# Decoder layer on one core: new places among the products for the small steps of twelve attention units, and other engines for some scalings and splits

## The chip, the cores and the metric

The kernel runs on one core of a Trainium2 chip. The metric is the device time of one execution in microseconds (us), lower is better. The core has five engines with a queue of instructions each: PE (TensorE, the products), DVE (VectorE), ACT (ScalarE), POOL (GpSimd) and SP (SyncE, which here starts the DMA transfers). Each engine takes its own instructions strictly in order and waits on semaphores for the others.

## The reference, cut to what matters

One decoder layer on x of 1024 tokens by 1024 channels, float32:

```python
h = rms_norm(x, ln_pre_mix)
proj = h @ w_in
u_pool, q, k, v = parts of proj            # 256 channels pooled, 12 heads of 64
q, k = rope(q, pos), rope(k, pos)
pool_out = multi_scale_pool(u_pool, w_pool, pool_scale)
for window, dilation in ((128, 1), (512, 4), (2048, 16)):
    o, lse = dilated_branch(q, k, v, window, dilation)   # blocks of 128, band of two blocks
attn_out = sum of the three o, weighted by softmax of the three lse
x = x + rms_norm(concat(pool_out, attn_out) @ w_out, ln_post_mix)
h = rms_norm(x, ln_pre_ffn)
x = x + rms_norm((silu(h @ w_gate) * (h @ w_up)) @ w_down, ln_post_ffn)
```

The change touches the attention alone, in the first 420 us or so. The feed-forward half behind it has the same instructions in the same order before and after.

## The kernel before

**Units.** The twelve heads are six pairs. A unit is a pair and a part h: units 0, 2, 4, 6, 8, 9 are h=0 of pairs 0 to 5 (the branch with dilation 4, called dense here, 5 score steps and 8 scalings), units 1, 3, 5, 7, 10, 11 are h=1 (the other two branches together, 8 score steps and 16 scalings). Each unit goes through the same stages:

- scores: PE makes q k products into a bank `ps_s`; DVE reduces the bank to the row maximum and leaves the shifted scores in the tile `pp` (L761 for dense, L827 for the rest); ACT takes exp (L764, L830).
- merge, for h=1 alone: DVE makes `ex` (L853), PE multiplies it by a selection matrix, and a chain of small DVE steps (L866 to L883) ends in the weights `wv`.
- weigh: each 128x256 piece of `pp` is multiplied by its weight, on DVE (L912), ACT (L910) or POOL (L914), as the table `wx` says (0 POOL, 1 DVE, 2 ACT). The dense units scale by `wd` (L770, then L894 to L898).
- turns: PE transposes four pieces of `pp` into a bank `ps_t` (L295); ACT copies it into `ptr` (L965), and DVE subtracts that copy from the bank (L966), which gives the low half.
- products: PE multiplies both halves of `ptr` by v into `ps_o`. At the end ACT takes the lower rows out (`low`, L1009), DVE adds them (L1010), and `mix` is written (L924, L926).

**Fill.** Between these steps PE does the projections of the pairs to come (`ps_pj`), three products for each 128 channels. The weight for them is split into a high half by ACT (L336) and a low half by DVE or POOL (L340; DVE in one instruction of 128x1024, POOL in two of 128x512), into tiles `whl`. What comes out of a projection of k or q is turned by position: a shuffle (L529) and a multiplication by cos (L530) on DVE, a multiplication by sin (L531) and an addition (L534) on DVE or POOL, then ACT and DVE split the result into `k` (L553, L554) or `qh` and `ql` (L559 to L561).

**What sets the order.** Every step of every unit has a place, a number: 5.4 lies four tenths of the way through unit 5. The table `PRM` (L30 on) holds the places by stage for h=0 and h=1 (`s0`, `s1` the scores, `m` the merge, `w0`, `w1` the weighing, `t0`, `t1` the turns, `v0`, `v1` the products), `du` adds a correction for each unit, and `emit` (L1135) runs all steps in order of place. PE's instructions keep the order in which they were written. For DVE, ACT and POOL a scheduler decides, with a priority for the steps inside `tc.high_priority`; how far ahead these are taken is `hp`, or the entry in `hk` for a stage ('s' reduce and exp, 't' the two halves of `ptr`, 'j' merge) and a unit. `we` says for each w_in tile which engine makes its low half, `r0` to `r3` and `rx` do so for the two multiplying and adding steps of a rotation.

PE has two banks for each of `ps_s`, `ps_t`, `ps_o` and `ps_pj`: a step that wants the third waits until the first has been read.

Of the kernel before, what the change touches and what calls it, by code (L numbers as in the profile page):

```python
# [28 lines left out]

PRM = {'sqe': (0, 0, 0, 0, 1, 1, 0, 1),  # L30
 'sqa': (1, 0, 0, 1, 0, 0, 0, 1),
 'we': (1, 1, 1, 0, 1, 0, 0, 0, 0, 0, 1, 0),
 'nt0': 0.55356,
 'nt1': 0.46388,
 'lag': 3.0,
 'hp': 150,
 'fl': 13,
 'lt': 2.819,
 'ls': 2.439,
 'lm': 2.915,  # L40
 'lw': (4.389, 0.132),
 'nm': 0.03805,
 'n2': 0.00854,
 'n0': 0.101,
 'n1': 0.37349,
 'h0': {'s0': -0.02534,
        's1': 0.41536,
        'm': 0.38673,
        'w0': 0.55,
        'w1': 0.95895,  # L50
        't0': 0.85,
        't1': 1.6,
        'v0': 1.1,
# [1 line left out]
 'h1': {'s0': 0.0,  # L55
        's1': 0.54775,
        'm': 0.61911,
        'w0': 0.77087,
        'w1': 1.33988,
        't0': 0.97415,  # L60
        't1': 1.84152,
# [2 lines left out]
        'u0': 0.15366,  # L64
        'u1': 0.10633,
        'u2': 0.41454,
        'u3': 0.53154},
 'f0': 7e-05,
 'f1': -0.00185,
 'first': {'s0': 0.526,  # L70
           's1': 0.6942,
           'm': 0.79582,
           'w0': 0.75,
           'w1': 0.95,
           't0': 1.09294,
           'v0': 1.3,
           'v1': 1.95},
 'vt': ((1.1002, 1.11456),
        (2.75936, 3.21636),
        (4.7781, 5.38909),  # L80
        (6.79523, 7.29364),
        (8.78599, 10.29739),
        (9.92992, 10.41018)),
 'pw': (-0.11865, -0.09, -0.01308),
 'wp': (1, 1, 1),
 'pb': 0.53585,
 'pe': 0,
 'cut': {7: (1, 12, 9), 9: (1, 10, 17)},
# [188 lines left out]
ON_DVE = ((0, 1),)  # L277
SWAP16 = [(i + 16) % 32 for i in range(32)]
# [1778 lines left out]
```

## Time and profile before

| | |
|---|---|
| median of 3 runs | 1110.48 us (1109.21 to 1111.19) |
| profiled execution | 1109.0 us, with a span of 1107.2 us from the first to the last instruction |
| TensorE clock granted in it | 0.999 |
| busy in the span | PE 99%, DVE 72%, ACT 50%, POOL 47% |

The profiled execution lies 1.5 us below the median and just under the lowest of the three runs. A row of the timeline has the start in us, the time from the first start to the last end of the row's instructions in us, the engine, the line, the operation, what it writes and reads, the shape, and the number of instructions (x4); a bracket at the end is idle time of the engine just ahead, and what ended it. Neighbouring products overlap: one of 128x512 is shown as 0.39 us long and the next starts 0.23 us after it. A row of the waits has the engine, what it was about to do, what it waited for, and then the sum, the number and the longest of these waits.

### The profile page before, as it was taken

How to read it: one execution, taken by the hardware profiler on the slowest of the kernel's cores; microseconds unless marked ns; L12 is line 12 of the kernel's file. 1: busy time of each engine (PE TensorE's matmuls, PEld its weight loads, DVE VectorE, ACT ScalarE, POOL GpSimd, SP SyncE). 2: the span in 40 equal slices, each digit the busy share in tenths (PEclk: the TensorE clock that was granted, in tenths of full speed). 3: DMA queues.
4: the chain of work that ended last, by engine and by line, in shares of the span. 5: the costliest groups of instructions: out<-in, count | busy, mean ns of one | idle time of the engine just before them, and what ended most of it. 6: DMA issues, size and time to landing. Idle time of an engine off the chain costs nothing.

```text
span 1107.2 us, 16032 instructions
## 1 busy us (share of the span) xinstructions
PE 1094.3 (99%) x5653; PEld 930.8 (84%) x5653; DVE 798.0 (72%) x1356; ACT 550.8 (50%) x985; POOL 524.8 (47%) x425
## 2 busy tenths in 40 slices
PE   9999999999999999999999999999999999999998
PEld 7888899989888888888888888888888888888887
DVE  7967978787988767799777777667566476343684
ACT  7456767676777755856322222233222535343432
POOL 0111617263554021100567777586568958666521
PEclk9999999999999999999999999999999999999999
DMA  8225232415149438664476666543445878656442
GB/s 296 95 75 189 95 136 71 159 67 181 53 158 338 146 144 305 226 228 154 158 241 238 238 238 232 205 171 124 152 177 210 281 274 286 205 180 206 134 152 77
DMA packets 91296, 201.81 MB, mean 182 GB/s; under 512 B 9296, under 2 KB 25168, under 8 KB 89808
## 3 DMA queue, kind: packets, MB, share of 16 engines
q1 hardware_dynamic: 90240, 200.00, 51.5%
q8 instruction: 44, 0.72, 0.3%
q10 hardware_dynamic: 976, 0.79, 0.2%
q14 instruction: 36, 0.29, 0.1%
HBM read 143.87 MB, written 56.89 MB: 181 GB/s over the span
## 4 chain that ended last, share of the span: by engine, by line
PE 90%; DVE 4%; ACT 3%; POOL 2%; issue 1%; DMA 0%; ACTq 0%; DVEq 0%; POOLq 0%
PE ps_pj L292 27%; PE ps_s L292 25%; PE ps_o L292 25%; PE ps_t L292 10%; PE ps_t L295 2%; POOL whl L340 1%; ACT ptr L965 1%; ACT pp L830 1%; DVE ptr L966 1%; DVE ql L561 0%; DMA wraw<-in_w_in_dram 0%; DVE pp L912 0%; DVE qh L560 0%; POOL rco L534 0%; DVE rsw L529 0%
## 5 line engine op out<-in xcount | busy, mean ns | idle before, releaser
L292 PE MATMUL ps_o<-tT,fw 128*128 128x512 f32 x648 | 150.4, 389 | 0.0
L292 PEld LDWEIGHTS ps_o<-tT,fw 128*128 128x128 f32 x648 | 121.6, 188 | 25.2
L292 PE MATMUL ps_pj<-x,whl 128*128 128x512 f32 x480 | 131.5, 399 | 0.2 <-DVE whl L340 0.2
L1482 POOL TENSOR_TENSOR fw<-rw,fw 128x512 fp32r<-128x512 f32 x72 | 99.0, 1398 | 32.1 <-ACT fw L1480 30.7
L292 PEld LDWEIGHTS ps_pj<-x,whl 128*128 128x128 f32 x480 | 86.4, 188 | 14.6 <-DVE whl L340 0.7
L340 POOL TENSOR_TENSOR whl<-wraw,whl 128x512 fp32r<-128x512 f32 x44 | 60.3, 1392 | 66.8 <-ACT whl L336 62.1
L1777 POOL TENSOR_TENSOR op<-rw,op 128x512 fp32r<-128x512 f32 x38 | 61.1, 1607 | 39.1 <-ACT op L1776 39.1
L366 POOL TENSOR_TENSOR nrr<-nrr,half 128x4 f32<-128x4 f32 (+1 forms) x7 | 6.9, 988 | 141.1 <-ACT eps L365 99.0
L292 PE MATMUL ps_s<-b,fw 128*128 128x512 f32 x312 | 72.5, 389 | 0.0
L1778 DVE TENSOR_TENSOR op<-rw,op 128x512 fp32r<-128x512 f32 x33 | 45.1, 1368 | 34.5 <-ACT op L1776 32.4
L1776 ACT ACTIVATE op<-rw 128x1024 fp32r<-128x1024 f32 x38 | 40.0, 1059 | 58.6 <-PE ps_t L292 28.6
L292 PEld LDWEIGHTS ps_s<-b,fw 128*128 128x128 f32 x312 | 58.6, 188 | 12.1
L1482 POOL TENSOR_TENSOR whl<-rw,whl 128x512 fp32r<-128x512 f32 x30 | 47.9, 1616 | 43.4 <-ACT whl L1480 29.6
L1480 ACT ACTIVATE fw<-rw 128x1024 fp32r<-128x1024 f32 x45 | 47.5, 1062 | 38.7 <-PE ps_o L292 15.5
L292 PE MATMUL ps_pj<-whl,x 128*128 128x256 f32 (+1 forms) x432 | 64.7, 298 | 0.0
L966 DVE TENSOR_TENSOR ptr<-ps_t,ptr 128x512 fp32r<-128x512 f32 (+1 forms) x84 | 53.0, 647 | 14.5 <-ACT ptr L965 14.1
L965 ACT ACTIVATE ptr<-ps_t 128x512 fp32r<-128x512 f32 (+1 forms) x84 | 45.3, 562 | 32.5 <-PE ps_t L295 23.7
L292 PEld LDWEIGHTS ps_pj<-whl,x 128*128 128x128 f32 x432 | 57.3, 191 | 2.2
L830 ACT ACTIVATE pp<-pp,sx 128x256 f32<-128x256 f32 x96 | 47.9, 501 | 8.1 <-DVE sx L827 7.6
L292 PE MATMUL ps_o<-ptr,v 128*128 128x128 f32 (+3 forms) x376 | 50.6, 268 | 1.2 <-DVE ptr L966 0.8
L1777 POOL TENSOR_TENSOR fw<-rw,fw 128x512 fp32r<-128x512 f32 x26 | 41.6, 1599 | 19.4 <-ACT fw L1776 18.8
L292 PE MATMUL ps_pj<-b,fw 128*128 128x512 f32 x216 | 50.3, 389 | 0.0
(337 smaller groups left out, 2773.9 us busy)
## 6 DMA issues: line engine op xcount, KB each, us to landing
rw<-bd SPq DMA_DIRECT2D x77, 256.0 KB, 4.1
rw<-in_w_gate_dram SPq DMA_DIRECT2D x28, 512.0 KB, 4.7
rw<-in_w_up_dram SPq DMA_DIRECT2D x28, 512.0 KB, 5.6
v<-vd SPq DMA_DIRECT2D x22, 512.0 KB, 4.6
rw<-wsd SPq DMA_DIRECT2D x44, 256.0 KB, 3.9
bd<-p SPq DMA_DIRECT2D x39, 256.0 KB, 2.1
rw<-in_w_down_dram SPq DMA_DIRECT2D x33, 256.0 KB, 4.2
wraw<-in_w_out_dram SPq DMA_DIRECT2D x15, 512.0 KB, 5.7
```

The source lines that it names most:

```text
L292: return tc.keep_in_program_order(nc.tensor.matmul(*a, **k))
L295: return tc.keep_in_program_order(nc.tensor.transpose(dst, src, by))
L340: pin(eng.tensor_tensor(dst[:, 1, at:at + w], src[:, at:at + w], dst[:, 0, at:at + w].bitcast(F32), ALU.subtract))
L366: powers.append(nc.gpsimd.tensor_tensor(r, r, half.to_broadcast([P, n]), ALU.pow))
L830: nc.scalar.activation(pt[:, j, lo:], pt[:, j, lo:], AF.Exp, bias=sx[:, 0, side, j, hd, 0:1], scale=-1.0, accum_out=sx[:, 0, side, j, hd, ...
L965: nc.scalar.activation(ptr[:, 0, :w], t[:, :w], AF.Copy)
L966: nc.vector.tensor_tensor(ptr[:, 1, :w], t[:, :w], ptr[:, 0, :w].bitcast(F32), ALU.subtract)
L1480: nc.scalar.activation(dst[:, :, 0], src, AF.Copy)
L1482: low[0] = eng.tensor_tensor(dst[:, i, 1], src[:, i], dst[:, i, 0].bitcast(F32), ALU.subtract)
L1776: nc.scalar.activation(w[:, :, 0], raw, AF.Copy)
L1777: nc.gpsimd.tensor_tensor(w[:, 0, 1], raw[:, 0], w[:, 0, 0].bitcast(F32), ALU.subtract)
L1778: (nc.gpsimd if p == "P1" else nc.vector).tensor_tensor(w[:, 1, 1], raw[:, 1], w[:, 1, 0].bitcast(F32), ALU.subtract)
```

## The change

Only the table `PRM` changes. Every function stays as it was, and PE does the same instructions, some of them in another order. The core of the diff:

```diff
- 'we': (1, 1, 1, 0, 1, 0, 0, 0, 0, 0, 1, 0),
+ 'we': (1, 1, 1, 1, 1, 0, 0, 0, 0, 0, 1, 0),
- 'hp': 150,
- 'fl': 13,
+ 'hp': 270,
+ 'fl': 17,
...
  'du': {3: {'v1': 0.155,
-            't0': 0.157,
+            't0': 0.128,
...
         6: {
-            'w0': 0.0776,
-            's1': 0.0406,
+            'w0': 0.0184,
+            's1': 0.0582,
...
         9: {
-            'v0': 0.279,
+            'v0': 0.3167,
...
         10: {
-             'm': 0.0548,
+             'm': -0.0026,
...
- 'r0': (1, 0),
- 'r1': (1, 0),
+ 'r0': (1, 1),
+ 'r1': (1, 1),
...
- 'wx': {3: {7: 2, 4: 2, 3: 0, 2: 2},
-        5: {9: 0, 15: 2, 13: 1, 12: 2, 14: 2, 10: 2},
+ 'wx': {3: {7: 2, 4: 2, 3: 2, 2: 2, 12: 1},
+        5: {9: 0, 15: 2, 13: 1, 12: 2, 14: 2, 11: 2, 1: 2},
...
-        10: {9: 2, 12: 0, 7: 0, 11: 2, 6: 1},
+        10: {9: 2, 12: 0, 7: 0, 11: 2, 6: 1, 1: 2, 8: 2, 13: 0},
...
- 'hk': {('s', 10): 450,
-        ('j', 7): 0,
+ 'hk': {('j', 7): 0,
...
- 'rx': {(1, 5, 1): (0, 1),
-        (1, 1, 1): (0, 1),
+ 'rx': {(1, 1, 1): (0, 1),
         (0, 2, 0): (0, 0),
         (1, 2, 1): (0, 1),
-        (0, 1, 1): (0, 1)},
+        (0, 1, 1): (0, 1),
+        (1, 1, 0): (0, 0)},
```

Besides, some forty places in `h0`, `h1`, `first`, `last`, `vt`, `c0` to `c3`, `ca`, `pn` and `du` get new numbers, most by a few hundredths of a unit; `sg` gets zeros in two places where it is not read, and the table `wd` of default engines gets new values in two places. In lines of the kernel after, everything behind the table stands four lines lower (L912 is L916 there).

By engine, over the whole program: the 128x256 scalings go from 27 to 18 on DVE, from 23 to 31 on ACT and from 46 to 47 on POOL. Unit by unit, as POOL/DVE/ACT: unit 1 from 9/5/2 to 10/3/3, unit 3 from 8/3/5 to 7/3/6, unit 5 from 6/4/6 to 6/2/8, unit 7 from 8/4/4 to 9/2/5, unit 10 from 8/5/3 to 8/2/6. One weight split of 128x1024 (w_in tile 3) goes from POOL to DVE. The sin multiplication of k of pair 1, first half, goes from DVE to POOL with its addition; for k of pair 5, second half, the multiplication goes to DVE and the addition to POOL. The two additions of the first pair's rotation go from POOL to DVE.

Three places show how instructions move. First DVE at the weighing of unit 5, ahead of the score reduces of unit 6 (`pp` weighed by `wv`, then the sin step `rsw`, then the reduce L761 of `ps_s`). Before:

```order
L529 STREAM_SHUFFLE rsw<-ps_pj 128x512
L530 TENSOR_TENSOR rco<-ps_pj,cosr 128x512
L912 TENSOR_SCALAR pp<-pp,wv 128x256 x4
L531 TENSOR_TENSOR rsw<-rsw,sinr 128x512
L761 ISA pp,sd<-ps_s,mD 128x512
```

and now:

```order
L533 STREAM_SHUFFLE rsw<-ps_pj 128x512
L534 TENSOR_TENSOR rco<-ps_pj,cosr 128x512
L916 TENSOR_SCALAR pp<-pp,wv 128x256 x2
L535 TENSOR_TENSOR rsw<-rsw,sinr 128x512
L765 ISA pp,sd<-ps_s,mD 128x512
```

Two of the four scalings have gone from DVE's queue; ACT has them now. At unit 7 the same stands two for four, there ahead of a weight split (L340) that PE's projection needs.

Second PE at the same place: the third score step of unit 6 (the rows of 128x256 into `ps_s`) among the projection `ps_pj`. Before:

```order
L292 MATMUL ps_pj<-x_120,whl 128x512 x3
L292 MATMUL ps_pj<-x_121,whl 128x512 x3
L292 MATMUL ps_s<-k,qh 128x256
L292 MATMUL ps_s<-k,ql_97 128x256
L292 MATMUL ps_s<-k,qh 128x256
L292 MATMUL ps_s<-k,ql_97 128x256
L292 MATMUL ps_pj<-x_122,whl 128x512 x3
L295 MATMUL ps_t<-idt,pp 128x128 x8
```

and now:

```order
L296 MATMUL ps_pj<-x_120,whl 128x512 x3
L296 MATMUL ps_pj<-x_121,whl 128x512 x3
L296 MATMUL ps_pj<-x_122,whl 128x512 x3
L296 MATMUL ps_s<-k,qh 128x256
L296 MATMUL ps_s<-k,ql_97 128x256
L296 MATMUL ps_s<-k,qh 128x256
L296 MATMUL ps_s<-k,ql_97 128x256
L299 MATMUL ps_t<-idt,pp 128x128 x8
```

The score step now stands behind three more products.

Third DVE in unit 1's products: the low half of `ptr`, and the low halves of `k` of pair 1. Before:

```order
L966 TENSOR_TENSOR ptr<-ps_t,ptr 128x512
L761 ISA pp,sd<-ps_s,mD 128x256
L761 ISA sd 128x1
L761 ISA pp,sd<-ps_s,mD 128x256
L761 ISA sd 128x1
L554 TENSOR_TENSOR k<-rcl,k 64x512 x2
L966 TENSOR_TENSOR ptr<-ps_t,ptr 128x512
L770 RECIPROCAL wd<-sd 128x4
```

and now:

```order
L970 TENSOR_TENSOR ptr<-ps_t,ptr 128x512
L765 ISA pp,sd<-ps_s,mD 128x256
L765 ISA sd 128x1
L765 ISA pp,sd<-ps_s,mD 128x256
L765 ISA sd 128x1
L970 TENSOR_TENSOR ptr<-ps_t,ptr 128x512
L558 TENSOR_TENSOR k<-rcl,k 64x512 x2
L774 RECIPROCAL wd<-sd 128x4
```

The second `ptr` has passed the two halves of `k`; ACT's queue has the same exchange (L965 ahead of the two L553).

Further moves that the prediction names, all on PE: unit 3's first turns stand ahead of a score step and three projection products that they followed, and its first products ahead of a score step and six products for v; the merge of unit 10 stands ahead of three projection products, three turns and two products that it followed; unit 9's first product follows three projection products and four turns that it preceded; and seven turns of unit 8 stand behind ten products of unit 7 instead of ahead of them.

More of the change, by code (lines that the diff above doesn't have):

```diff
@@ L31 @@
  'sqa': (1, 0, 0, 1, 0, 0, 0, 1),
- 'we': (1, 1, 1, 0, 1, 0, 0, 0, 0, 0, 1, 0),
+ 'we': (1, 1, 1, 1, 1, 0, 0, 0, 0, 0, 1, 0),
  'nt0': 0.55356,
- 'nt1': 0.46388,
+ 'nt1': 0.4474,
  'lag': 3.0,
- 'hp': 150,
- 'fl': 13,
+ 'hp': 270,
+ 'fl': 17,
  'lt': 2.819,
@@ L42 @@
  'nm': 0.03805,
- 'n2': 0.00854,
- 'n0': 0.101,
+ 'n2': -0.11451,
+ 'n0': 0.11471,
  'n1': 0.37349,
@@ L47 @@
         's1': 0.41536,
-        'm': 0.38673,
-        'w0': 0.55,
-        'w1': 0.95895,
+        'm': 0.38372,
+        'w0': 0.54475,
+        'w1': 1.02727,
         't0': 0.85,
@@ L57 @@
         'm': 0.61911,
-        'w0': 0.77087,
+        'w0': 0.77023,
         'w1': 1.33988,
@@ L66 @@
         'u2': 0.41454,
-        'u3': 0.53154},
+        'u3': 0.49482},
  'f0': 7e-05,
@@ L70 @@
  'first': {'s0': 0.526,
-           's1': 0.6942,
+           's1': 0.67082,
            'm': 0.79582,
-           'w0': 0.75,
+           'w0': 0.71719,
            'w1': 0.95,
@@ L78 @@
  'vt': ((1.1002, 1.11456),
-        (2.75936, 3.21636),
-        (4.7781, 5.38909),
+        (2.73517, 3.20352),
+        (4.80938, 5.38909),
         (6.79523, 7.29364),
         (8.78599, 10.29739),
-        (9.92992, 10.41018)),
+        (9.81568, 10.37567)),
  'pw': (-0.11865, -0.09, -0.01308),
```

137 rows, old and new, of the table PRM are left out of this document.

## The prediction

> **What bounds the kernel now.** I read the page first, then the windows, then PE's waits, and then the timeline at each wait. The engines:
>
> ```profile
> PE 1094.3 (99%) x5653; PEld 930.8 (84%) x5653; DVE 798.0 (72%) x1356; ACT 550.8 (50%) x985; POOL 524.8 (47%) x425
> ```
>
> PE is busy for 1094.3 of 1107.2 us, so whatever the other engines save reaches the end only where PE stands still, 12.9 us in all. Where that is, the windows tell:
>
> ```profile
> 200.00:250.00 50.00, 48.50 (x327) 44.27 (x326) 41.82 (x111) 35.87 (x88) 22.85 (x25) 1.00 0.31 107
> ...
> 400.00:450.00 50.00, 50.00 (x257) 42.32 (x255) 35.76 (x48) 30.02 (x51) 7.55 (x5) 1.00 0.67 251
> ```
>
> Behind the attention PE is busy for the whole of a window; in the attention a window lacks up to 2 us. What PE waited for between 20 and 420 us:
>
> ```profile
> PE ps_s L292 <- DVE sd L761: 1.5, 1, 1.5
> PE ps_s L292 <- DVE ex L853: 1.1, 1, 1.1
> PE ps_o L292 <- DVE ptr L966: 0.8, 2, 0.5
> PE ps_o L292 <- DVE dhl L1112: 0.8, 1, 0.8
> PE ps_s L292 <- ACT z L1298: 0.4, 1, 0.4
> PE ps_pj L292 <- DVE whl L340: 0.2, 1, 0.2
> PE ps_o L292 <- ACT pp L830: 0.2, 1, 0.2
> ```
>
> Eight waits, 5.0 us, and nearly all on DVE, which is 72% busy: it comes late in single places, not on the whole. The idle time understates a delay: a product that runs out still counts as busy past the usual start of the next, by 0.39 - 0.23 = 0.16. Below I take the late start. So the change is worth what becomes of these places, and what new ones arise.
>
> **The change part by part.**
>
> *Unit 5's scalings and unit 6's third score step (the 1.5).* DVE, POOL and PE there:
>
> ```profile
> 225.75 2.02 DVE L912 TENSOR_SCALAR pp<-pp,wv 128x256 f32<-128x256 f32 x4
> 227.69 1.76 DVE L531 TENSOR_TENSOR rsw<-rsw,sinr 128x512 f32<-128x512 f32 x1
> 229.38 0.68 DVE L761 CUSTOM_DVE_ANT_0 pp<-ps_s,mD 128x512 f32<-128x512 f32 x1
> ```
>
> ```profile
> 224.77 2.86 POOL L914 TENSOR_SCALAR pp<-pp,wv 128x256 f32<-128x256 f32 x6 [4.05 <-DVE wv L883]
> 227.59 3.00 POOL L340 TENSOR_TENSOR whl<-wraw,whl 128x512 fp32r<-128x512 f32 x2
> ```
>
> ```profile
> 227.30 1.32 PE L292 MATMUL ps_pj<-x,whl 128*128 128x512 f32 x5
> 230.12 0.39 PE L292 MATMUL ps_s<-k,qh 128*128 128x256 f32 x1 [1.50 <-DVE sd L761]
> ```
>
> Five products at 0.23 us end their turn at 228.45; the score step starts at 230.12, 1.67 late, because its bank is read by the reduce L761 only until 230.06. The four scalings take 2.02, 0.5 each, so two fewer take 1.0 off DVE's queue: L531 starts at about 226.7. There it meets POOL's scalings (2.86 for six, 0.48 each) and not the split L340 that began at 227.59 and beside which L531 took 1.76. Amid POOL's scalings at 283.63 (below) it took 0.67. So L761 starts at 227.4, or 227.9 if L531 waits for one of POOL's scalings, and ends by 228.6. The score step comes three products later, at 228.45 + 0.68 = 229.13. It doesn't wait: gain 1.67, and 0.5 us to spare. ACT has two scalings more, at 0.50:
>
> ```profile
> L910 ACT ACTIVATE pp<-pp,wv 128x256 f32<-128x256 f32 x23 | 9.9, 499 | 4.5 <-DVE wv L883 4.4
> ```
>
> They end 1.0 later, and ACT's next work there is the exp behind L761: hidden.
>
> [...]
>
> *Unit 1's scalings and the order of `ptr` and `k` (the two of 0.8).*
>
> ```profile
> 114.47 1.47 DVE L912 TENSOR_SCALAR pp<-pp,wv 128x256 f32<-128x256 f32 x3
> ...
> 120.02 0.69 DVE L966 TENSOR_TENSOR ptr<-ps_t,ptr 128x512 fp32r<-128x512 f32 x1
> ```
>
> ```profile
> 125.07 1.40 DVE L554 TENSOR_TENSOR k<-rcl,k 64x512 fp32r<-64x512 f32 x2
> 126.51 0.69 DVE L966 TENSOR_TENSOR ptr<-ps_t,ptr 128x512 fp32r<-128x512 f32 x1
> ```
>
> ```profile
> 119.46 0.99 PE L292 MATMUL ps_o<-ptr,v 128*128 128x128 f32 x9
> 120.76 0.44 PE L292 MATMUL ps_o<-ptr,v 128*64 128x128 f32 x3 [0.31 <-DVE ptr L966]
> ```
>
> ```profile
> 125.99 0.75 PE L292 MATMUL ps_o<-ptr,v 128*128 128x256 f32 x5
> 127.25 0.56 PE L292 MATMUL ps_o<-ptr,v 128*64 128x256 f32 x4 [0.52 <-DVE ptr L966]
> ```
>
> Product 9 of the first row starts at 120.18 and its partner, due 0.1 later, at 120.76: 0.5 late. DVE's rows between the two above follow each other without a bracket, and two of the three scalings leave (1.47/3 = 0.49 each): `ptr` starts 1.0 earlier, at 119.0, and is done by 119.7. Gain 0.5. ACT's one scaling more (0.50) delays its half of `ptr`, for which DVE's row has no wait either. At 127.25 the product is 0.67 late, behind two halves of `k` (1.40) which `ptr` now passes: gain 0.7. What is late next is `k`, by 0.69; it is the second half of pair 1, which unit 3 reads first, a stage later.
>
> *Unit 7's scalings (the 0.2 on L340).*
>
> ```profile
> 281.77 1.94 DVE L912 TENSOR_SCALAR pp<-pp,wv 128x256 f32<-128x256 f32 x4
> 283.63 0.67 DVE L531 TENSOR_TENSOR rsw<-rsw,sinr 128x512 f32<-128x512 f32 x1
> 284.23 1.41 DVE L340 TENSOR_TENSOR whl<-wraw,whl 128x1024 fp32r<-128x1024 f32 x1
> ```
>
> ```profile
> 285.70 0.50 PE L292 MATMUL ps_pj<-x,whl 128*128 128x512 f32 x1 [0.23 <-DVE whl L340]
> ```
>
> The split ends 1.0 earlier, at 284.7, and the product, 0.23 + 0.16 = 0.4 late, no longer waits. POOL gets a ninth scaling, so its addition for `k` behind it ends some 0.5 later; that `k` is of a pair whose scores start two stages on. Gain 0.4.
>
> *Unit 8's turns.*
>
> ```profile
> 304.12 2.68 PE L292 MATMUL ps_pj<-x,whl 128*128 128x512 f32 x11
> 306.92 1.14 PE L295 MATMUL ps_t<-pmt,pp 128*128 128x128 f32 x7
> ```
>
> ```profile
> 306.17 1.29 DVE L966 TENSOR_TENSOR ptr<-ps_t,ptr 128x512 fp32r<-128x512 f32 x2
> ```
>
> The turns start 0.3 late and lose 0.2 more within, since DVE reads their two banks until 306.86 and 307.46. The ten products of unit 7 that now come first read what these very instructions write. Only their low halves need it, so about 0.3 remains: gain 0.2.
>
> *Unit 9's first product.*
>
> ```profile
> 342.44 0.71 PE L292 MATMUL ps_o<-ptr,v 128*128 128x512 f32 x2 [0.17 <-ACT pp L830]
> ```
>
> ```profile
> v<-vd SPq DMA_DIRECT2D x1, 512.0 KB, 6.8
> ```
>
> The first row is PE's, the second the transfer's, from the view of DMA issues in the window 335.3 to 335.9. The waits name ACT, but v, issued at 335.5, took 6.8 to land and was there at 342.3 only; the product is 0.17 + 0.16 = 0.3 late. Three projection products and four turns (1.1 us) now stand before it. Its place in SP's queue is the same. Gain 0.3.
>
> *What stays.* The waits on L853 (unit 1's merge), L1112 (the pooled channels) and L1298 have the same instructions ahead of them on their engines; the split of w_in tile 3 falls into a gap of DVE. I take zero for these, with 0.5 either way.
>
> *What may be new.* Unit 3's products stand 1.3 us earlier on PE, and DVE there has
>
> ```profile
> 174.91 2.18 DVE L534 TENSOR_TENSOR rcl<-rco,rsw 128x512 f32<-128x512 f32 x1
> ```
>
> ```profile
> 177.01 1.25 DVE L966 TENSOR_TENSOR ptr<-ps_t,ptr 128x512 fp32r<-128x512 f32 x2
> ```
>
> ```profile
> 178.91 1.49 PE L292 MATMUL ps_o<-ptr,v 128*128 128x128 f32 x16
> ```
>
> The addition holds up `ptr`, whose two parts are done at 177.7 and 178.3. Eight products read each part, and from 1.3 earlier, 177.6, the first eight run as soon as the first part is there, and the second eight at 178.3: a wait of 0.1. If the addition has to let another half of POOL's split pass (3.00/2 above), it is up to 1.5. The merge of unit 10 stands 1.5 earlier; the nearest row is unit 1's merge, 1.1 above. Bounds 0 and 2.6; I take 0.6, nearer to zero, since POOL has one scaling (0.48) less ahead of its split at unit 3 than before.
>
> *Sum.* 1.67 + 0.5 + 0.7 + 0.4 + 0.2 + 0.3 = 3.8, less 0.6: 3.2 us. The profiled execution, 1109.0, becomes 1105.8. It lies 1.5 below the median of the runs, 1110.5, so the median becomes 1107.3.
>
> **The rivals.** A measurement of this kernel can tell about 0.2%, 2.2 us, from no change.
>
> [...]
>
> *The waits come back elsewhere.* PE arrives earlier everywhere behind 120 us, while DVE keeps 72% of work, so other places with little to spare turn into waits: with the bound of 2.6 in place of 0.6 the gain is 1.2: 1109.3, no change. For it: eight waits, all but one single, each at another instruction, so the next candidates aren't in view.
>
> *Slower.* Collisions of DVE and POOL of the kind in the 1.76 row, 1.1 us each (1.76 - 0.67). Their place is unit 3, where L534 precedes a `ptr` wanted earlier, and every place where POOL's queue moved. Six that hit a path without slack take 3.8 + 2.2 us and more: 1113. Against it: in the attention DVE's seven L531 of this kind hold one such collision, and POOL gets no more work.
>
> *It does more.* The waits on L853 and L1112 shrink too, as DVE has 0.5 us less before the first: 1105.
>
> **How the numbers follow.** Forecast (1106 to 1108.3) 0.50; port 0.12; waits elsewhere 0.20; slower 0.08; more 0.10. Faster by over 0.2% (below 1108.3) is the forecast, the last case and a third of the port case: 0.64. Within 0.2%: two thirds of the port case and the waits elsewhere, 0.28. Slower 0.08. The range leaves out the slower case and the far ends of the others: 1104.5 to 1111.
>
> **What would show it.** PE's waits between 20 and 420 us sum to about 2.7 instead of 5.0; the row on L761 and both on L966 in unit 1 are gone, those on L853, L1112 and L1298 stay. DVE's L531 at about 227 takes under 1.2. PE's busy time stays at 1094 and the windows behind 420 us are the same. The prediction is wrong if new rows with `ps_s` or `ps_o` at units 3, 4, 8 or 10 stand in the waits with a sum over 1.5, or if L761 at unit 6 stays.

## The result and the profile after

| | before | after |
|---|---|---|
| median | 1109.85 us (6 runs, 1108.64 to 1111.19) | 1103.88 us (6 runs, 1103.11 to 1106.30) |
| profiled execution, span | 1109.0, 1107.2 | 1103.1, 1101.3 |
| ratio | | 0.995, 95% interval 0.9937 to 0.9962 |

The change takes 6.0 us off. Forecast were 3.2 off, 1107.3, with a range from 1104.5 to 1111: the direction is right, the gain nearly twice as large, and the time lies below the range. (The six runs of before have a median 0.6 lower than the three that the forecast started from.) In the lines of the kernel after, everything stands four lower (L761 is L765).

The first line of the page and the waits of PE between 20 and 420 us, after:

```profile
PE 1091.4 (99%) x5653; PEld 930.7 (85%) x5653; DVE 796.7 (72%) x1350; ACT 553.8 (50%) x994; POOL 519.9 (47%) x421
```

```profile
PE ps_o L296 <- DVE dhl L1116: 0.8, 1, 0.8
PE ps_s L296 <- DVE ex L857: 0.5, 1, 0.5
PE ps_s L296 <- ACT z L1302: 0.4, 1, 0.4
```

Three waits of 1.7 us stand where eight of 5.0 stood. DVE is as busy as before; its work only comes in time. PE's busy time fell by 2.9, though it does the same products: a product that runs out counts as busy past the usual start of the next (by 0.39 less 0.23 us at 512 columns), so the idle time, 12.9 before and 9.9 after, shows only half of the gain. The window around the largest wait, from the view of windows (after the window's length PE, PEld, DVE, ACT and POOL busy, then the clock):

```profile
200.00:250.00 50.00, 50.00 (x347) 46.16 (x345) 40.17 (x110) 37.01 (x89) 22.44 (x24) 1.00 0.35 120
```

347 products lie in it where 327 did. The place itself, unit 6's third score step, in DVE's, POOL's and PE's timeline after:

```profile
223.53 1.04 DVE L916 TENSOR_SCALAR pp<-pp,wv 128x256 f32<-128x256 f32 x2
224.49 0.67 DVE L535 TENSOR_TENSOR rsw<-rsw,sinr 128x512 f32<-128x512 f32 x1
225.08 0.68 DVE L765 CUSTOM_DVE_ANT_0 pp<-ps_s,mD 128x512 f32<-128x512 f32 x1
```

```profile
222.55 3.33 POOL L918 TENSOR_SCALAR pp<-pp,wv 128x256 f32<-128x256 f32 x6 [4.04 <-DVE wv L887]
225.85 2.55 POOL L344 TENSOR_TENSOR whl<-wraw,whl 128x512 fp32r<-128x512 f32 x2
```

```profile
224.78 2.29 PE L296 MATMUL ps_pj<-x,whl 128*128 128x512 f32 x9
226.91 0.28 PE L296 MATMUL ps_s<-k,qh 128*128 128x256 f32 x1
```

L535 takes 0.67 while POOL is still at its scalings, the reduce ends at 225.76, and the score step at 226.91 has no bracket: L535 wasn't held up here.

Below, a late start is the distance from a product's start to the next one's, less the usual distance for its width (0.227 us for 512 columns, 0.119 for 256). Summed over the program they are 5.9 us less after than before, which is the difference of the spans. Where PE's order is the same in two kernels, product can be laid beside product, and a difference has a place. A place has one trace for each kernel, while the times are medians of several executions, so the two needn't agree to the tenth.

### The profile page after: what moved, and what is told of

It reads as the page before. It is cut to its first block, busy times and chain, and to the rows that moved or that the text cites. A ratio compares the mean times of both kernels' runs of the same rounds, so it can differ in the third digit from the quotient of the medians.

```text
span 1101.3 us, 16033 instructions
## 1 busy us (share of the span) xinstructions
PE 1091.4 (99%) x5653; PEld 930.7 (85%) x5653; DVE 796.7 (72%) x1350; ACT 553.8 (50%) x994; POOL 519.9 (47%) x421
## 4 chain that ended last, share of the span: by engine, by line
PE 97%; ACT 1%; DVE 1%; DMA 0%; issue 0%; POOL 0%; ACTq 0%; DVEq 0%
PE ps_pj L296 31%; PE ps_s L296 26%; PE ps_o L296 26%; PE ps_t L296 10%; PE ps_t L299 3%; DMA wraw<-in_w_in_dram 0%; ACT pp L834 0%; PE ps_o L299 0%; ACT ptr L969 0%; ACT z L1302 0%; POOL rcl L538 0%; POOL rsw L535 0%; ACT whl L340 0%; DVE y L1899 0%; ACT k L557 0%
## 5 line engine op out<-in xcount | busy, mean ns | idle before, releaser
L344 POOL TENSOR_TENSOR whl<-wraw,whl 128x512 fp32r<-128x512 f32 x42 | 57.4, 1389 | 49.7 <-ACT whl L340 41.0
```

Source lines behind the costliest of these rows:

```text
L344: pin(eng.tensor_tensor(dst[:, 1, at:at + w], src[:, at:at + w], dst[:, 0, at:at + w].bitcast(F32), ALU.subtract))
```

## The experiments

The tables of the change fall into four groups: **W**, the engines of the scalings (`wx`, `wd`); **A**, the engines of rotations and of the weight split (`r0`, `r1`, `rx`, `we`); **P**, all places; **K**, the priorities (`hp`, `hk`). W, A and K leave PE's order as it is. All kernels below are before or after with some of the tables exchanged; their lines are numbered as before. Twelve kernels ran, each against before on its chip.

**One place alone: two scalings of unit 5 to ACT.**

```diff
-        5: {9: 0, 15: 2, 13: 1, 12: 2, 14: 2, 10: 2},
+        5: {9: 0, 15: 2, 13: 1, 12: 2, 14: 2, 10: 2, 1: 2, 4: 2},
```

> The kernel before, with two entries of wx alone changed: pieces 1 and 4 of unit 5 are scaled by ACT instead of DVE. PE's order stays. Theory (DVE's queue sets L761 at unit 6): L531 starts at about 226.7 instead of 227.69, takes under 1.2 in place of 1.76, and the reduce L761 ends by 228.6, so the third score step, which PE reaches at 228.45, is at most 0.15 late instead of 1.67. Time: 1.5 to 1.7 us less than before, nothing at other places over 0.3. [...] Rival (the waits come back elsewhere): the row on L761 goes, but new late products behind 230 take 1 us or more back.

Measured: 1112.39, ratio 1.0025 (1.0016 to 1.0033): slower. The step itself came out to the hundredth: the score step is 0.00 late where it was 1.67. But further on there is a new wait, at unit 6's products. First DVE there before, then the waits, and DVE's, POOL's and PE's timeline with the two scalings on ACT:

```profile
238.80 1.29 DVE L966 TENSOR_TENSOR ptr<-ps_t,ptr 128x512 fp32r<-128x512 f32 x2 [0.41 <-ACT ptr L965]
...
240.84 0.86 DVE L560 CAST qh<-rco 64x512 fp32r<-64x512 f32 x2
```

```profile
PE ps_o L292 <- DVE ptr L966: 4.0, 4, 3.0
```

```profile
237.08 2.87 DVE L560 CAST qh<-rco 64x512 fp32r<-64x512 f32 x2
239.98 1.41 DVE L561 TENSOR_TENSOR ql<-rco,qh 64x512 fp32r<-64x512 f32 x2
...
242.11 1.28 DVE L966 TENSOR_TENSOR ptr<-ps_t,ptr 128x512 fp32r<-128x512 f32 x2
```

```profile
234.92 1.60 POOL L534 TENSOR_TENSOR rco<-rco,rsw 128x512 f32<-128x512 f32 x1
236.48 3.19 POOL L340 TENSOR_TENSOR whl<-wraw,whl 128x512 fp32r<-128x512 f32 x2
```

```profile
242.85 1.22 PE L292 MATMUL ps_o<-ptr,v 128*64 128x256 f32 x9 [2.99 <-DVE ptr L966]
```

Two scalings fewer let the scheduler set a rotation's addition (L534) ahead of the split on POOL, and with `rco` ready earlier it put the CASTs and subtractions of `qh` and `ql` ahead of `ptr` on DVE, and two reduces too. There the CASTs lie beside POOL's split and take 1.43 each instead of 0.43. The product that reads `ptr` is 3.15 late. So the relief paid 1.67 and the new order cost 3.15: the rival that the waits come back, at a price above the bound of 2.6 that I gave it. The rest of what this trace lost is 0.3 at unit 9 and a late start of 1.3 at 603 us (last section).

**The same with unit 6's places.**

```diff
-         6: {'m': -0.2027, ..., 'w0': 0.0776, 's1': 0.0406, ..., 't1': 0.1828},
+         6: {'m': -0.2434, ..., 'w0': 0.0184, 's1': 0.0582, ..., 't1': 0.1597},
```

> Pieces 1 and 4 of unit 5 on ACT as in the run that moved them alone, and unit 6's corrections (du, entry 6) as after: its third score step stands three products later on PE. In DVE's queue the halves of unit 6's ptr then stand ahead of the steps of qh and ql again, as before; in the run with the two pieces alone they stood behind them and behind two reduces, and PE waited 3.0 for them. Theory (the loss there was the order of DVE's queue, which shifts when work leaves it, not the relief itself): the wait on L761 (1.5) is gone, the wait of 3.0 on L966 at unit 6 isn't there, the CASTs L560 of that place take 0.42 each: 1.4 to 1.9 us less than before. Rival (POOL's split and DVE meet at this place whatever the order, so that the relief always comes back later): L966 at unit 6 waits 1 us or more, and the time is within 0.5 of before.

Measured: 1108.26, ratio 0.9987 (0.9978 to 0.9996), 1.4 less than before; span 1105.6, 1.6 less. DVE at that place:

```profile
237.23 1.29 DVE L966 TENSOR_TENSOR ptr<-ps_t,ptr 128x512 fp32r<-128x512 f32 x2 [0.41 <-ACT ptr L965]
...
239.26 0.86 DVE L560 CAST qh<-rco 64x512 fp32r<-64x512 f32 x2
```

`ptr` first, the CASTs at 0.43 each behind the split and the addition on POOL: the theory held. The places of the change do more than move products; through the scheduler they decide what DVE does in which order. This kernel takes the bad order and the collision away together, so it doesn't say what each is worth.

**Is it the order, or the collision?** The two CASTs of the slow place (the 15th and 16th of their line) go to ACT, in the kernel with the two scalings alone:

```diff
-                pin(nc.vector.tensor_copy(hi[oth, a], c[own]))
+                did('qh'); pin((nc.scalar.copy if seen['qh'] in (15, 16) else nc.vector.tensor_copy)(hi[oth, a], c[own]))
```

> The kernel with pieces 1 and 4 of unit 5 on ACT (1.5 behind at unit 6 through ptr, 3.15 late), with one more edit: the two CASTs of unit 6's qh that stood beside POOL's split and took 1.42 and 1.43 are made by ACT. PE's and POOL's order stay; DVE loses the two CASTs there, and one subtraction for ql moves behind two reduces. [...] Rival (the order of the queue alone is the price, and the CASTs' length beside POOL doesn't matter): 2 x 0.42 less, ptr 2.3 late. [...]

Measured: 1110.34, ratio 1.0006 (0.9997 to 1.0015), 2.1 less than with the CASTs on DVE. Of these 2.1 at most 1.6 are from this place: two products are 0.90 and 0.65 late, 1.55 in place of 3.15, and not the 2.3 of the order alone. Part of the 1.55 is now ACT's, which does the CASTs ahead of its half of `ptr`, and a subtraction beside the split takes 1.55 in place of 0.7:

```profile
PE ps_o L292 <- ACT ptr L965: 0.7, 1, 0.7
PE ps_o L292 <- DVE ptr L966: 0.4, 1, 0.4
```

```profile
237.22 1.55 DVE L561 TENSOR_TENSOR ql<-rco,qh 64x512 fp32r<-64x512 f32 x1
```

By the rows of the kernel with the two scalings alone, the CASTs' stretch, 2.87 for 0.86, is 2.0 of the 3.15, and the order the other 1.1. This run takes the stretch away and puts ACT's and the subtraction's delays in its place; what it shows is that 1.6 of the price goes when the CASTs leave DVE, more than the 0.9 that the order alone would give back. In ten traces (before, after, and the first eight kernels here) 54 of the 240 CASTs of this kind began while a POOL instruction was running: 53 of them took 0.59 to 1.43. The last one, and all of the other 186, took 0.42 to 0.43. So beside a running POOL instruction a CAST took up to 1.43 against 0.43; why, these runs don't show. My prediction had reckoned with such a stretch at L531 (1.76 against 0.67) and L534, and not at the CASTs.

**The groups alone.** W:

> The kernel before, with the engines of the scalings (the tables wx and wd) as after and all else as before. PE's order is the same; DVE's queue at unit 1 has ptr ahead of the split of k already. Theory (each place is on its own): the waits on L761 at unit 6 (1.5) and on both L966 at unit 1 (0.8) and the one on L340 at unit 7 (0.2) are gone, late starts 1.67 + 0.5 + 0.7 + 0.4 less: 3.3 us, over half of the 6.0 that the whole change brought; the wait on L853 stays at 1.1. Rival (the groups need each other: PE's new order makes the room): under 2 us. Rival (the extra 2.7 us beyond the prediction come from the scalings too, through many short delays): 4.5 us or more.

Measured: 1111.58, ratio 1.0016 (1.0008 to 1.0025). Late starts fall by 0.47 and 0.68 at unit 1, 1.67 at unit 6, 0.39 at unit 7, 0.27 at unit 8, so the theory's places are right (that of unit 8 wasn't in it). `ptr` at unit 6 takes 3.17 back. PE's clock is 0.50 for 6.8 us about that wait, another 2.8, and new late starts stand at 323 (0.57), 326 (0.34) and 631 (1.41). The profiled execution, 1113.6, is the slowest of its eleven, so not all have all of that. None of the three expectations had a loss; the third, that the scalings bring the excess, is out.

A:

> The kernel before, with the engines of the rotations and of one weight split (r0, r1, rx, we) as after and all else as before. PE does the same products in the same order. At unit 1 the sin step of k (L531) leaves DVE's queue ahead of the last reduces L827. Theory (the wait on unit 1's merge, L853, was set by that queue): the reduces there end about 0.4 earlier relative to PE, the wait on L853 falls from 1.1 to 0.5 or 0.6, and the time by 0.4 to 0.7 us; the other seven waits stay. Rival (the merge became earlier because of the places on PE or of the other scalings): the wait stays at 1.1 and the time the same within 0.2.

Measured: 1108.63, ratio 0.9988 (0.9980 to 0.9997). PE, and its row in the waits:

```profile
107.19 0.43 PE L292 MATMUL ps_s<-ex,ls 128*128 128x64 f32 x2 [0.55 <-DVE ex L853]
```

The merge is 0.77 late in place of 1.34, the size that the theory gave; a turn at 104 is 0.27 late that wasn't. So the place is worth 0.30, and the section on the prediction says how. Behind the first 10 us no other place on PE differs by more than 0.12, so the trace explains 0.3 of the 1.2 by which the median is lower, which the interval allows.

P:

> The kernel before, with the places of the steps alone as after (h0, h1, du, first, last, vt and the rest); the engines of scalings, rotations and splits and the priorities are as before. Theory (each place is on its own): the late starts at units 8, 9 and 10, 0.5 at 306, 0.3 at 342, 0.3 around 358, 0.2 at 346, are gone and so are some shorter ones between 50 and 200; the waits on L761 at unit 6, and L966 at unit 1, stay as the engines ahead of them keep their work: 1.5 to 2.2 us less than before. Rival (the score step of unit 6, now three products later on PE, has 0.68 less to wait even with four scalings ahead): 0.7 more, 2.2 to 2.9. Rival (places alone expose other waits, since DVE has not been relieved): no gain or a loss.

Measured: 1112.18, ratio 1.0020 (1.0011 to 1.0029). PE's waits, and DVE and POOL at unit 8:

```profile
PE ps_o L292 <- DVE ptr L966: 3.4, 4, 2.3
...
PE ps_o L292 <- DMA v<-vd: 1.1, 1, 1.1
PE ps_s L292 <- DVE sd L761: 0.8, 1, 0.8
```

```profile
299.60 2.84 DVE L560 CAST qh<-rco 64x512 fp32r<-64x512 f32 x2
```

```profile
299.00 3.16 POOL L340 TENSOR_TENSOR whl<-wraw,whl 128x512 fp32r<-128x512 f32 x2
```

The step of unit 6 has 0.98 left, as three products later must leave; but at unit 8 the same thing happens that happened at unit 6, two CASTs beside a split, and `ptr` is 2.4 late. The third expectation, a new wait, was the right one.

**Each group left out of after.**

> After without its new places: scalings, rotations, splits and priorities as after, the places of the steps, and so PE's order, as before. Theory (the engines' share and the places need each other): the waits on L761 at unit 6, L966 at unit 1, L340 are gone (3.6 us of late starts) and the one on L853 is 0.6, but ptr at unit 6 is 3 us late, as in the run with the scalings alone, and unit 8 to 9 add 0.5 to 0.9: 0 to 1.5 us slower than before. Rival (the groups add up: places are worth the remaining 2 us only): 3.5 to 4.5 us faster than before.

Measured: 1110.31, ratio 1.0002 (0.9994 to 1.0011). The places priced at units 1, 6, 7 and 8 are served, and 0.57 at the merge, but the two waits

```profile
PE ps_o L292 <- DVE ptr L966: 3.0, 1, 3.0
PE ps_o L292 <- DMA v<-vd: 1.5, 1, 1.5
```

eat it up. In the profiled execution, the slowest of its eleven at 1111.7, the late starts of these two are 3.12 and 1.83, and a clock of 0.50 behind each costs 1.7 and up to 1.5. The theory held.

> After without its new engines for the scalings (wx and wd as before): places, rotations, splits, priorities as after. Theory (they need each other): the late starts of the run with the places alone come again, 0.5 and 0.7 at unit 1, 1.0 at unit 6, 0.4 at the split before unit 7's scores, 2.4 at unit 8 behind two CASTs of DVE beside a POOL split, 1.3 at unit 9; only L853 is 0.57 shorter: 1.5 to 2.5 us slower than before. Rival (the groups add up): 2.0 to 2.6 us faster than before.

Measured: 1110.17, ratio 1.0011 (0.9999 to 1.0022). The late starts of P alone are back, 0.47, 0.67, 0.98, 0.39 and 2.48, and smaller ones of 0.34 at 190 and 0.19 at 288, while those on the merge and on v are not: 5.5 behind after at these places, 6.3 in the medians. I expected 1.5 to 2.5 more than before; the medians are 0.2 apart, and the ratio's interval reaches to 2.4. In the trace v came in time, where P alone waited 1.1 for it.

> After with the rotations and the weight split on the engines of before (r0, r1, rx, we). Theory (the shorter wait on unit 1's merge comes from the sin step of k that left DVE's queue, and from nothing else): the wait on L853 is 1.1 again in place of 0.5, 0.3 to 0.6 us slower than after, all else as after. Rival (these too need the rest): a new wait of 1 us or more somewhere behind 120 us.

Measured: 1105.44, ratio 0.9964 (0.9951 to 0.9978), 1.6 slower than after, with intervals that overlap. The profiled execution, 1108.1, is the slowest of its five, and 1.6 of that lie in its first 50 us: products start 0.43 apart until 11.1 there, in after until 4.6. In it the merge is 0.57 later again; late starts of 0.42 and 0.47 on two weight splits, at 318 and 321, are new, and

```profile
PE ps_o L292 <- DMA v<-vd: 1.4, 1, 1.4
```

So the theory's size holds for the merge, but not its "all else as after". The one wait of over 1 us is v's, which may be chance (last section).

K was not run by itself. Alone, or together with the other three, it changes DVE's order at two places, where reduces pass a `ptr`, ACT's at one, and POOL's and PE's not at all; what that is worth wasn't measured.

**Two numbers more.** The rest of after's waits, tried one by one.

```diff
- 'pn': (..., (1.0234, 1.03879, 1.16807)),
+ 'pn': (..., (1.005, 1.03879, 1.16807)),
```

> After, with one number changed: the pooled means of the second channel half for the first 512 tokens (pn) at 1.005 in place of 1.0234, eight products earlier on PE, so that the two steps that follow each other at 87 us are apart and the last one finds its bank ps_o read. Theory: the wait on the pooled channels' dhl (late start 0.96) falls to 0.3 or less, all else as after: 0.6 to 0.9 us faster than after. Rival (DVE's queue changes its order behind it, as at unit 6): unit 1's merge or a ptr behind it comes 0.5 us or more late, no gain.

Measured: 1103.56, ratio 0.995 (0.9937 to 0.9962). The wait on `dhl` is gone, 0.96 less; 0.32 came up at the products behind it and 0.11 at the merge: about 0.5 net in the trace, too small for the times to show.

```diff
-        1: {..., 'm': -0.0274, ...},
+        1: {..., 'm': -0.0074, ...},
```

> After, with one number changed: unit 1's merge 0.02 later, which puts one more product of 0.23 ahead of it on PE. Theory (each place on its own): the wait on L853 falls from 0.77 late to 0.54, the time by 0.2. Rival (the order of DVE and POOL changes behind it: at unit 2 a sin step now stands ahead of a split on POOL, and qh's CASTs stand earlier on DVE): a new late start of 0.5 to 3 us between 106 and 140, slower than after.

Measured: 1109.08, ratio 0.9993 (0.9984 to 1.0002): one merge one product later, and 5.2 of the 6.0 us are lost. The step `ex` in after, then DVE, POOL and PE at unit 1 here:

```profile
106.01 0.23 DVE L857 TENSOR_TENSOR ex<-sx,qdA 128x64 f32<-128x64 f32 x1 [0.29 <-ACT pp L834]
```

```profile
106.05 0.72 DVE L529 STREAM_SHUFFLE rsw<-ps_pj 128x512 f32<-128x512 f32 x1
106.67 0.67 DVE L530 TENSOR_TENSOR rco<-ps_pj,cosr 128x512 f32<-128x512 f32 x1
107.26 1.00 DVE L853 TENSOR_TENSOR ex<-sx,qdA 128x64 f32<-128x64 f32 x1
```

```profile
106.91 1.26 POOL L531 TENSOR_TENSOR rsw<-rsw,sinr 128x512 f32<-128x512 f32 x1 [6.83 <-DVE rsw L529]
```

```profile
108.31 0.69 PE L292 MATMUL ps_s<-ex,ls 128*128 128x64 f32 x2 [2.14 <-DVE ex L853]
```

A shuffle and a product by cos now stand ahead of `ex`, which itself takes 1.00 instead of 0.23, beside a sin step of POOL; then the clock is 0.50 for 3.4 us, and at unit 2 products that read `ptr` are 1.15 and 0.55 late. The rival was right.

Last, the first number together with unit 11's last score place 0.02 later, which leaves the other engines' orders alone:

```diff
-         11: {...},
+         11: {..., 's1': 0.02},
```

> After, with two numbers changed: the pooled means at 1.005 as in the run with that one number, and unit 11's last score place (du, entry 11, s1) 0.02 later. The second puts three more products of the output projection, 3 x 0.23 = 0.69, ahead of the score step that waits for ACT to read its bank (z, L1298: late starts 0.62 + 0.23 + 0.15 at 364 in the trace of after); DVE's, ACT's and POOL's orders are the same as with the first number alone. Theory (a place can be bought back alone where no queue changes its order): the row on z is gone, 0.6 to 1.0 us less there, 1.0 to 1.5 us less than after together, 1102.4 to 1102.9. Rival (the score steps behind it come too late for DVE's reduces, unit 11's merge waits instead): the same or slower than after, 1103.5 to 1105.

Measured: 1104.11, ratio 0.995 (0.9936 to 0.9963). PE's waits:

```profile
PE ps_o L292 <- DVE sq L1665: 0.8, 1, 0.8
PE ps_s L292 <- DVE ex L853: 0.7, 1, 0.7
PE ps_s L292 <- DVE sx L827: 0.4, 2, 0.2
```

The row on z is gone, and the score steps behind it now wait for DVE's reduces: nothing gained. The second expectation was right. Neither of the two beats after by more than the times can tell.

## Why the prediction was right or wrong

Each term of the sum, against the late starts at its place before and after:

| step of the prediction | predicted | measured | shown by |
|---|---|---|---|
| unit 5's scalings, L761 | 1.67 | 1.67 | two scalings alone |
| unit 1, both L966 | 0.5 + 0.7 | 0.47 + 0.68 | W alone |
| unit 7's split, L340 | 0.4 | 0.39 | W alone |
| unit 8's turns | 0.2 | 0.27 | the two traces; W alone has it too |
| unit 9's first product | 0.3 | 0.52 | the two traces |
| what stays (L853, L1112, L1298) | 0 | 0.57 on L853 | A alone, A left out |
| what may be new | -0.6 | -0.27 | A alone |
| not in the sum | | 0.49: unit 3's products at 190 (0.29) and unit 9's at 347 (0.20) | the two traces |
| not in the sum | | 1.1, in delays under 0.2 each | the remainder of 5.9 |

*Right*: the bound, and the four places on DVE. Every one came out within 0.1, with the reason given (two scalings fewer, `ptr` past `k`). L531 took 0.67, L1112 and L1298 kept their rows. At unit 8 the size is right, but not the reason: the turns lose their delay in W alone too, where they stand in their old place, so the move on PE isn't needed for it.

*Wrong, step "what stays"*: I said that L853 has the same instructions ahead of it on its engine, and put its gain at nothing. It measured 0.57, and the order ahead of it is another. ACT and DVE at unit 1 before:

```profile
101.60 1.27 ACT L553 ACTIVATE k<-rcl 64x512 fp32r<-64x512 f32 x2
```

```profile
101.25 0.69 DVE L966 TENSOR_TENSOR ptr<-ps_t,ptr 128x512 fp32r<-128x512 f32 x1 [0.26 <-ACT ptr L965]
```

and with A alone, where PE is 0.68 later up to there:

```profile
100.82 1.28 ACT L553 ACTIVATE k<-rcl 64x512 fp32r<-64x512 f32 x2 [0.70 <-POOL rcl L534]
```

```profile
103.95 0.69 DVE L966 TENSOR_TENSOR ptr<-ps_t,ptr 128x512 fp32r<-128x512 f32 x1
```

With group A the sin step of `k` stands on POOL just ahead of its addition, which ends 0.49 earlier against PE (at 100.78, less 0.68, for 100.59). ACT then takes the two halves of `k` ahead of `ptr` instead of behind it, in time in which it had stood idle; from there its queue runs without a break up to the exps that `ex` waits for, and these and `ex` come 0.28 earlier. The last reduces come only 0.22 earlier, so the reason in my expectation for A alone, 0.4 off DVE's queue, was not it: DVE stood idle for 0.55 behind the sin step before. The other half of the 0.57 is no gain: `ptr` on DVE goes behind both halves of `k`, 2.0 later, a turn waits 0.27 for its bank, and PE comes to the merge that much later. The -0.27 in the table is this turn, and the two rows together are worth 0.30. Which of A's four tables does it was not tried one by one. My rival "it does more" named the wait on L853, for DVE's relief, and I gave it 0.10. The diff showed the sin step going to POOL, and I didn't carry it to the wait behind it.

*Wrong, step "what may be new"*: 0.6 was mis-sized, 0.27 came, at the turn at 104 us just named. The places that I feared, unit 3 and unit 10, have no wait.

*Wrong, the sum's reach*: I priced only what the list of waits shows. 1.6 us lay in places without a row in it, 0.29 at 190, 0.20 at 347, and 1.1 in pieces too small to name. This is the largest part of the miss. The 0.29 goes with the scalings: it is gone in all three kernels that have W and another group, 0.17 of it is left with W alone, and without W 0.20 to 0.41 stand there. The rest I can't assign to a group, so its cause stays open. Unit 9's product was mis-sized: it is not only no longer late but has 0.08 in hand. That rests on v landing in 6.7 us in the trace of after; in the one without A it took 9.2, and the product in its new place was 1.6 later.

These make 0.33 + 0.57 + 0.22 + 0.07 + 0.49 + 1.1, less 0.06 for the rounding of the others: 2.7, the distance from 3.2 to 5.9. The time itself lies 3.4 below the forecast, since before's median is 0.6 lower over six runs.

*The rival "the waits come back"* had its chance, 0.20, for a good reason, and was mis-sized as well: with the places alone, with the scalings alone, and with either left out, it is what happens, at 2.4 to 3.2 us a place. After's order, from places and scalings together, is free of it. Unit 6, where it strikes with the scalings, was not among the places that I named, and unit 8 only in the list of signs: I read DVE's order in after, and no order of a part.

No run shows the port that the forecast names with a chance of 0.12. What the traces show of L531 at this place is 1.76 beside POOL's split before, and 0.67 amid POOL's scalings after.

## What to carry to other kernels

Where a scheduler sets an engine's order from places and priorities, price a place from the trace, but read the order of the whole kernel: a part of such a change can lose what the whole gains, and one number 0.02 further cost 5.2 us. List, for every wait that is said to stay, what the change takes out of the queue ahead of it, on all engines. And look where DVE's copies and two-input steps will lie beside POOL's long instructions: here a CAST took up to 1.43 for 0.43, and L531 1.76 for 0.67. A pair of such CASTs cost 2.0, and the wait that had been removed 1.67.

## What the runs showed of the hardware

**Four of seven long waits of PE had a clock of 0.50 behind them.** In the kernel with unit 1's merge moved, the view of windows behind the wait of 2.14 (clock in the third column from the end):

```profile
109.00:110.00 1.00, 1.00 (x3) 0.70 (x4) 0.82 (x4) 0.00 (x0) 0.52 (x1) 0.50 0.00 0
...
112.00:114.00 2.00, 2.00 (x11) 1.64 (x10) 1.87 (x5) 0.00 (x0) 0.00 (x0) 1.00 0.00 0
```

Products start 0.43 apart instead of 0.23. Behind 15 us the traces hold seven late starts of 1.8 us or more; four were followed by such a stretch, which cost 1.5 to 2.8 against the same products in before or after; three were not. By the clock column three of the stretches last 3.4 us and one 6.8. Late starts of 1.83 and 2.36 were enough, while one of 3.15, with the two scalings alone, had a clock of 1.00 behind it; what decides, no run shows.

**The same transfer differs by 2.5 us between traces.** v for unit 9, from the view of DMA issues, in the kernel without A:

```profile
v<-vd SPq DMA_DIRECT2D x1, 512.0 KB, 9.2
```

against 6.8 before and 6.7 after. Without P it is issued at 335.5 as in before, behind the same transfers at the same times, and takes 8.2. So a kernel whose first product stands some seven microseconds behind the issue had it 0 to 1.8 late. Each kernel has one trace, so whether it differs as much between executions of one kernel isn't shown. Perhaps of the same kind is the wait on `sq` (L1665, a transfer to memory that it overwrites) at 590 to 650 us, 0.5 to 1.2 in six of the traces and none in before and after, where every engine does the same instructions; why it came in these, the runs don't tell.
